# Another order at the last turns, in the first tail and before the first MLP group of a decoder block in Strassen-Winograd form

## The chip, the cores and the metric

The kernel runs on one core of a Trainium2 chip. The metric is the device time in microseconds, the median of several executions. The engines are TensorE (PE in the profile: matrix products and transposes), VectorE (DVE), ScalarE (ACT), GpSimd (POOL) and SyncE (SP). SP and POOL also issue the DMA transfers, each in a queue of its own that works in order.

## The reference

One layer (`DEPTH = 1`) on 512 tokens of width 2048, all float32. What matters, cut to its lines:

```python
h = rmsnorm(x, g_mix[l])
z = jnp.einsum('bsd,dc->bsc', h, w_in[l])
cb, cc, cv, q, k, v, f_logit, gate_c, gate_a = jnp.split(z, SPLIT_POINTS, axis=-1)
conv_y = cb * causal_dwconv(cc * cv, conv_w[l])
conv_branch = jnp.einsum('bsc,cd->bsd', conv_y, w_conv_out[l])
attn_branch = jnp.einsum('bsc,cd->bsd', forgetting_attention(q, k, v, log_f), w_attn_out[l])
merged = gc * conv_branch + ga * attn_branch
x = x + jnp.einsum('bsd,de->bse', merged, w_mix_out[l])
h = rmsnorm(x, g_mlp[l])
u = jnp.square(jax.nn.relu(jnp.einsum('bsd,df->bsf', h, w_ff1[l])))
x = x + jnp.einsum('bsf,fd->bsd', u, w_ff2[l])
return rmsnorm(x, g_final)
```

## The kernel before

**Products.** Every large product is done in 2 x 2 blocks with seven block products instead of eight, named A11, A12, S1, S2, S3, S4 and A22. Their operands are blocks or sums of blocks, of the activations (made once and kept as `ST`, `Q1`, `Q2` or `M`) and of the weights (made on VectorE for each group, lines L125 and L128). Each operand is split in a high part (a copy to a shorter format on ScalarE, `high_of`, L111, tiles `th`) and a low part (the rest, a subtraction on VectorE, `low_of`, L114, tiles `tl`). A block product is three rounds of matmuls: high by high, high by low, then low by high; so TensorE wants the high part of the weights at once and their low part after two thirds of the product (`mm_cols`) or of its first half (`mm_rows`).

**Groups.** A `Group` is one set of output columns. It loads four weight blocks X[i, j] of 1 MB each. `head` does A11 and A12, `tail`, `tail2` and `tail3` the other five in different orders. `run` splits an operand, queues its matmuls and then calls what is entered for that product in `after`. Four weight buffers x0 to x3 are passed on through the list `free`; two buffers each serve `th` and `tl`.

**Order.** The instructions are written in program order, and a planner then orders each engine's queue: of the instructions that are ready by its simulated times it takes the earliest in the program. `tied` (while `strict` is set) and `tc.keep_in_program_order` pin an instruction behind everything written before it on its engine; `tc.issue_after(i)` puts what follows behind `i` on i's engine, without waiting for its end. An engine executes its queue in the planner's order, whatever is ready on the chip.

**The three places.** (1) At the start, the rows of x come in four blocks `xin[0..3]`. Blocks 2 and 3 are scaled by their norm's factors r2 and r3 (made on GpSimd, L649; scaled at L731 and L732), turned by 32 transposes in eight steps of four (`turn_both`, L542, over the PSUM banks 6, 7, 2, 5), and copied out with the gain by `gained_both` (L550 on VectorE, L552 on ScalarE). Then the first key group's A11 begins. (2) The first group, `gV0`, has done A11 and A12 by then; its tail comes after the key groups' heads. Into it falls the split of the activations' S4 operand, `fourth`, entered behind S3. (3) The output projection's last group (g = 3, `tail3`) is followed by the first MLP group `g0`, whose weights come through GpSimd's queue (`g0.ahead`). Behind each product of the last group stand steps: `g0.ahead(i, j)` loads a block; `begin_part(n, k)` loads the first six eighths of an activation operand, which wait in memory; `split_part` splits A11's and A12's. `mix.first_of`, `mix.sums` and `mix.out` make the last two eighths of S1, S3, S2, S4 and A22 from the last group's own turned output. The lines that change there are these:

```python
g0.after = Steps(A11=[lambda: g0.ahead(1, 1), turn_waiting, begin_rest, lambda: first_sum_after(mix.added), mix.first_of],
                 A12=[lambda: mix.out("S1", mix.s1), mix.sums, lambda: factors(common, turned)])
```

Of the kernel before, what the change touches and what calls it, by code (L numbers as in the profile page):

```python
# [8 lines left out]
F32 = mybir.dt.float32  # L9
# [36 lines left out]
def tile_hybrid_block(ctx: ExitStack, tc, x, g_mix, w_in, b_f, b_gate, conv_w, w_conv_out,  # L46
# [69 lines left out]
    def split(src, hi, lo):  # L116
        return high_of(src, hi), low_of(src, hi, lo)

    def split_in_order(*how):

        for i in split(*how):
            tc.keep_in_program_order(i)

    def sub(out, a, b):
        return nc.vector.tensor_tensor(out=out, in0=a, in1=b, op=ALU.subtract)  # L125

    def add(out, a, b):
        nc.vector.tensor_tensor(out=out, in0=a, in1=b, op=ALU.add)  # L128

    def parts(shape, at=0):  # L130

# [72 lines left out]
    class Group:  # L204
# [3 lines left out]
        def __init__(self, view, c1, c2, w, ST, mm, banks, put, scale=1.0, extra={}, after=None, shift=SHIFT):  # L208
            self.extra, self.after, self.shift = extra, {} if after is None else after, shift
            self.view, self.cs, self.w, self.ST, self.mm, self.banks = view, (c1, c2), w, ST, mm, banks  # L210
            self.put, self.scale, self.at = put, scale, {}
            self.begun, self.queue, self.X = False, nc.sync, {}
            self.pinned, self.mid, self.apart, self.ready = False, {}, False, {}
            self.nq = view.shape[0] // (2 * P)

        def load(self, i, j):
# [12 lines left out]
            return [bank(i, which) for i in self.banks["abcd".index(which)]]  # L229

        def run(self, ps, n, src, first):
            if n in self.ready:
                hi, lo = self.ready.pop(n)
            else:
                hi, lo = self.places()
                split(src, hi, lo)
            if n in self.mid:
                self.mm(ps, self.ST(n), hi, lo, first, blocks=(0,))
                self.mid[n]()
                self.mm(ps, self.ST(n), hi, lo, first, blocks=(1,))  # L240
# [19 lines left out]
        def plus(self, s, ps, scale=1.0):  # L260

            if len(ps) == 1:
                pairs = [(s, ps[0][:, :2 * self.w].rearrange("p (b c) -> p b c", b=2))]
            else:
                pairs = [(s[:, b, :], ps[b][:, :self.w]) for b in range(2)]
            for o, p in pairs:
                if scale == 1.0:
                    add(o, p, o)
                else:
                    nc.vector.scalar_tensor_tensor(out=o, in0=p, scalar=scale, in1=o, op0=ALU.mult, op1=ALU.add)  # L270

        def done(self, *ij):
            free.append(self.at.pop(ij))
# [75 lines left out]
        def first_sum(self, pinned=True):  # L349
# [4 lines left out]
            if pinned:  # L354
                tc.keep_in_program_order(one)

        def tail2(self):

            X = self.quarters((0, 1), (0, 0), (1, 1), (1, 0))
            a = self.a  # L360
            if not self.pinned:
                sub(X[0, 0], X[0, 1], X[0, 0])
            c = self.acc("c")
            self.run(c, "S1", X[0, 0], True)
            third = sub(X[0, 1], X[1, 1], X[0, 1])
            if self.pinned:
# [4 lines left out]
            sub(X[two], X[1, 1], X[0, 0])  # L371
            self.done(*other)
            d1 = self.snap(d, self.scale, (1, 1))
            self.plus(d1, c, self.scale)
            while later:
                later.pop(0)()
            self.run(a, "S2", X[two], False)
            sub(X[1, 0], X[1, 0], X[two])
            self.done(*two)
            s2 = self.snap(a, ij=(1, 0))  # L380
            self.plus(d1, a, self.scale)
            self.put(1, 1, d1)
            self.run(c, "S4", X[1, 1], False)
            self.done(1, 1)
            s4 = self.snap(c, self.scale, (0, 1))
            self.plus(s4, a, self.scale)
            self.put(0, 1, s4)
            self.run(d, "A22", X[1, 0], False)
            self.done(1, 0)
            self.plus(s2, d)  # L390
            self.put(1, 0, s2)


        def tail3(self):

            X = self.quarters((0, 1), (0, 0), (1, 1), (1, 0))
            a = self.a
            sub(X[0, 0], X[0, 1], X[0, 0])
            c = self.acc("c")
            self.run(c, "S1", X[0, 0], True)  # L400
            sub(X[0, 0], X[1, 1], X[0, 0])
            d1 = self.snap(c)
            self.run(a, "S2", X[0, 0], False)
            sub(X[1, 0], X[1, 0], X[0, 0])
            self.done(0, 0)
            s2 = self.snap(a)
            self.plus(d1, a)
            self.run(c, "S4", X[1, 1], False)
            sub(X[0, 1], X[1, 1], X[0, 1])
            self.done(1, 1)  # L410
            s4 = self.snap(c)
            self.plus(s4, a)
            self.put(0, 1, s4)
            d = self.acc("d")
            self.run(d, "S3", X[0, 1], True)
            self.done(0, 1)
            self.plus(d1, d)
            self.put(1, 1, d1)
            self.plus(s2, d)
            self.run(a, "A22", X[1, 0], True)  # L420
            self.done(1, 0)
            self.plus(s2, a)
            self.put(1, 0, s2)

# [65 lines left out]
    class Quarters:  # L490
# [51 lines left out]
                    tied(nc.tensor.transpose(pt[:, k, e * P:(e + 1) * P], xin[t][:, c * P:(c + 1) * P], ident))  # L542
            return pt

        def gained_both(self, i, cs, pt):

            for k, c in enumerate(cs):
                o, g = self.H[i, k][:, c // 2, :], self.gT[:, c:c + 1]
                if c & 2:
                    tied(nc.vector.tensor_scalar(out=o, in0=pt[:, k, :], scalar1=g, scalar2=None, op0=ALU.mult))  # L550
                else:
                    tied(nc.scalar.activation(out=o, in_=pt[:, k, :], func=AF.Copy, scale=g))  # L552

        def sums(self):
            H = self.H
# [172 lines left out]
    high_of(*A12[:2])  # L728
    low_of(*A12)
    tied(nc.scalar.activation(out=cols[:, KT:], in_=pv[:, :NV - KT], func=AF.Copy))  # L730
    tied(nc.vector.tensor_scalar(out=xin[2], in0=xin[2], scalar1=r2, scalar2=None, op0=ALU.mult))  # L731
    tied(nc.scalar.activation(out=xin[3], in_=xin[3], func=AF.Copy, scale=r3))  # L732
# [7 lines left out]
    Q1.tiles("A22")  # L740
    for n in range(KT // 2):
        cs = (2 * n, 2 * n + 1)
        Q1.gained_both(1, cs, Q1.turn_both((2, 3), cs, (6, 7, 2, 5)[n % 4]))
    low_of(keys.X[0, 0], hi3, lo3)
    keys.ready["A12"] = hi4, lo4 = keys.places()
    high_of(keys.X[1, 0], hi4)
    low_of(keys.X[1, 0], hi4, lo4)
    strict[0] = False
    s1 = gV0.snap(gV0.a)
    gV0.plus(s1, b)  # L750
    gV0.done(0, 0)
    gV0.done(1, 0)
    gV0.put(0, 0, s1)
# [11 lines left out]
        Q1.last_sum("S4", (0, 1))  # L765
        strict[0] = False

    gV0.after["S3"] = fourth
    for g in heads:
        g.tail2()  # L770
        if g is gV0:
# [157 lines left out]
    n = 0  # L929
# [273 lines left out]

    def split_part(n):
        lo = Q2[n][:, 1, :KT // 2 - 2]
        split_in_order(lo.bitcast(F32), Q2[n][:, 0, :KT // 2 - 2], lo)

    class Mix:

# [58 lines left out]

        def first_of(self):
            self.s1 = pm.tile([P, 2, HS], F32, tag="s1", name="s1")  # L1270
            add(self.s1, self.F[1][:, 0], self.F[1][:, 1])

        def sums(self):
            (a11, a12), (a21, a22) = ([f[:, par] for par in range(2)] for f in self.F)
            s1 = self.s1
            sub(a21, a11, a21)
# [90 lines left out]
    for g in range(4):  # L1367
# [16 lines left out]
            after.add("S2", mix.fourth)  # L1384
        else:
            after.add("A12", lambda: begin_part("A11", 0))
            after.add("S4", lambda: g0.ahead(0, 0), lambda: begin_part("S1", 1))
            after.add("S4", lambda: split_part("A11"))
            after.add("S3", lambda: g0.ahead(1, 0), lambda: begin_part("S3", 3))
            after.add("A22", lambda: g0.ahead(0, 1))  # L1390
            after.add("A22", lambda: split_part("A12"))
        group = groups[g]
# [2 lines left out]
            after.add("A11", group.first_sum)  # L1395
        if g == 3:
            group.mid["A22"] = turn_first
        group.head(True, between=groups[1].first if g == 0 else lambda: None)
        (group.tail2 if g < 3 else group.tail3)()
        before = mix  # L1400

    def begin_rest():
        for n, k in (("S2", 5), ("S4", 6), ("A22", 2)):
            begin_part(n, k)

    def first_sum_after(ins):
        with tc.issue_after(ins.ins):
            g0.first_sum(pinned=False)

    def factors(common, r):  # L1410

# [267 lines left out]
```

## Time and profile before

| | us |
|---|---|
| runs (3), lowest, median, highest | 2431.68, 2435.55, 2437.17 |
| profiled execution, device time | 2433.25 |
| its span, first to last instruction | 2431.4 |
| TensorE busy | 2404.7 |
| VectorE busy | 2041.5 |
| ScalarE busy | 1201.7 |
| GpSimd busy | 299.4 |

A row of the order of time begins with the start and the length in us, then engine, line, operation, out<-in, shape and count; in brackets stands the idle time of the engine before it and what ended it. A row of the list of waits has the waiting instruction, what it waited for, the sum in us, how often, and the longest. A row of a table of stretches has the stretch, its length, each engine's busy time with its instructions in brackets (PE, weight loads, DVE, ACT, POOL), the granted TensorE clock as a share of full speed, the DMA engines' mean share and their GB/s. A row of the DMA issues ends with the KB of one and the us from issue to landing.

### The profile page before, as it was taken

How to read it: one execution, taken by the hardware profiler on the slowest of the kernel's cores; microseconds unless marked ns; L12 is line 12 of the kernel's file. 1: busy time of each engine (PE TensorE's matmuls, PEld its weight loads, DVE VectorE, ACT ScalarE, POOL GpSimd, SP SyncE). 2: the span in 40 equal slices, each digit the busy share in tenths (PEclk: the TensorE clock that was granted, in tenths of full speed). 3: DMA queues.
4: the chain of work that ended last, by engine and by line, in shares of the span. 5: the costliest groups of instructions: out<-in, count | busy, mean ns of one | idle time of the engine just before them, and what ended most of it. 6: DMA issues, size and time to landing. Idle time of an engine off the chain costs nothing.

```text
span 2431.4 us, 41446 instructions
## 1 busy us (share of the span) xinstructions
PE 2404.7 (99%) x17783; PEld 2262.7 (93%) x17783; DVE 2041.5 (84%) x1739; ACT 1201.7 (49%) x1230; POOL 299.4 (12%) x480
## 2 busy tenths in 40 slices
PE   9999999999999999999999999999999999999998
PEld 9999999999999999899899999999998888888886
DVE  7987777788887778888889889898887888889898
ACT  6444434445555534356566666666665333333334
POOL 1100111111111112023300000000011001100000
PEclk9999999999999999999999999999999999999999
DMA  8564554464656755657855565655678567655662
GB/s 265 181 201 147 151 160 139 139 193 150 203 186 199 241 176 191 208 177 236 306 200 188 203 231 190 230 180 210 220 291 290 169 225 243 224 202 184 237 228 101
DMA packets 279847, 491.98 MB, mean 202 GB/s; under 512 B 11820, under 2 KB 191112, under 8 KB 279280
## 3 DMA queue, kind: packets, MB, share of 16 engines
q1 hardware_dynamic: 226384, 272.71, 35.5%
q0 software_dynamic: 52672, 215.57, 24.2%
q8 instruction: 139, 2.28, 0.4%
q10 hardware_dynamic: 608, 1.06, 0.1%
q14 instruction: 44, 0.36, 0.0%
HBM read 379.70 MB, written 109.07 MB: 201 GB/s over the span
## 4 chain that ended last, share of the span: by engine, by line
PE 86%; DVE 5%; issue 3%; DMA 3%; ACT 1%; POOL 1%; SPq 0%; DVEq 0%; POOLq 0%; ACTq 0%
PE a L165 6%; PE a L169 6%; PE a L167 6%; PE a L188 5%; PE d L165 5%; PE a L186 5%; PE a L184 5%; PE d L167 5%; PE d L169 5%; PE c L165 4%; PE c L167 4%; PE c L169 4%; PE d L188 3%; PE d L186 3%; PE d L184 3%
## 5 line engine op out<-in xcount | busy, mean ns | idle before, releaser
L111 ACT ACTIVATE th<-x 128x2048 fp32r<-128x2048 f32 (+1 forms) x280 | 536.8, 1918 | 508.2 <-DVE x L125 160.4
L114 DVE TENSOR_TENSOR tl<-x,th 128x2048 fp32r<-128x2048 f32 (+2 forms) x282 | 639.0, 2271 | 165.4 <-ACT th L111 154.4
L125 DVE TENSOR_TENSOR x<-x,x 128x2048 f32<-128x2048 f32 (+1 forms) x160 | 365.6, 2285 | 26.4 <-DMA x<-in_w_in_dram 18.9
L111 ACT ACTIVATE th<-y 128x2048 fp32r<-128x2048 f32 (+1 forms) x109 | 185.4, 1702 | 274.1 <-PE a L186 138.8
L114 DVE TENSOR_TENSOR tl<-y,th 128x2048 fp32r<-128x2048 f32 (+1 forms) x109 | 218.8, 2012 | 30.0 <-ACT th L111 29.5
L184 PE MATMUL a<-th,us 128*128 128x512 f32 x512 | 199.3, 389 | 1.0 <-ACT th L111 1.0
L186 PE MATMUL a<-th,us 128*128 128x512 f32 x512 | 199.2, 389 | 0.0
L165 PE MATMUL c<-S,th 128*128 128x256 f32 x848 | 196.4, 277 | 0.6 <-ACT th L111 0.6
L167 PE MATMUL c<-S,th 128*128 128x256 f32 x848 | 196.5, 277 | 0.0
L165 PE MATMUL a<-S,th 128*128 128x256 f32 x784 | 181.3, 277 | 0.0
L167 PE MATMUL a<-S,th 128*128 128x256 f32 x784 | 180.8, 277 | 0.0
L165 PEld LDWEIGHTS c<-S,th 128*128 128x128 f32 x848 | 159.4, 188 | 0.7 <-ACT th L111 0.7
L167 PEld LDWEIGHTS c<-S,th 128*128 128x128 f32 x848 | 159.4, 188 | 0.2 <-issue 0.2
L167 PEld LDWEIGHTS a<-S,th 128*128 128x128 f32 x784 | 147.3, 188 | 0.0
L165 PEld LDWEIGHTS a<-S,th 128*128 128x128 f32 x784 | 147.2, 188 | 0.0
L188 PE MATMUL a<-tl,us 128*128 128x512 f32 x512 | 136.9, 389 | 0.6 <-DVE tl L114 0.6
L165 PE MATMUL d<-S,th 128*128 128x256 f32 x544 | 127.4, 279 | 0.0
L167 PE MATMUL b<-A,th 128*128 128x256 f32 x544 | 127.4, 279 | 0.0
L167 PE MATMUL d<-S,th 128*128 128x256 f32 x544 | 126.9, 278 | 0.0
L165 PE MATMUL a<-A,th 128*128 128x256 f32 x544 | 126.8, 278 | 0.0
L165 PE MATMUL b<-A,th 128*128 128x256 f32 x544 | 126.1, 277 | 0.0
L167 PE MATMUL a<-A,th 128*128 128x256 f32 x544 | 126.1, 277 | 0.0
(398 smaller groups left out, 6063.7 us busy)
## 6 DMA issues: line engine op xcount, KB each, us to landing
x<-in_w_in_dram SPq DMA_DIRECT2D x86, 1024.0 KB, 6.2
y<-in_w_ff_dram SPq DMA_DIRECT2D x64, 1024.0 KB, 7.7
x<-in_w_ff_dram SPq DMA_DIRECT2D x60, 1024.0 KB, 8.3
us<-s_d POOLq DMA_DIRECT2D x48, 1024.0 KB, 9.3
s_d<-rh POOLq DMA_DIRECT2D x32, 896.0 KB, 5.5
s_d<-r POOLq DMA_DIRECT2D x32, 896.0 KB, 6.1
x<-in_w_mix_out_dram SPq DMA_DIRECT2D x17, 1024.0 KB, 7.0
g_d<-o POOLq DMA_DIRECT2D x32, 256.0 KB, 2.7
```

What stands on the lines that cost most here:

```text
L111: return tied(nc.scalar.activation(out=hi, in_=src, func=AF.Copy))
L114: return tied(nc.vector.tensor_tensor(out=lo, in0=src, in1=hi.bitcast(F32), op=ALU.subtract))
L125: return nc.vector.tensor_tensor(out=out, in0=a, in1=b, op=ALU.subtract)
L165: nc.tensor.matmul(o, hi[:, q, js], Sh, start=first and q == 0 and j == 0, stop=False, skip_group_check=True)
L167: nc.tensor.matmul(o, hi[:, q, js], Sl, start=False, stop=False, skip_group_check=True)
L169: nc.tensor.matmul(o, lo[:, q, js], Sh, start=False, stop=q == nq - 1, skip_group_check=True)
L184: tied(nc.tensor.matmul(o, Sh, hi[:, q, :], start=begin and q == 0, stop=False, skip_group_check=True))
L186: tied(nc.tensor.matmul(o, Sl, hi[:, q, :], start=False, stop=False, skip_group_check=True))
L188: tied(nc.tensor.matmul(o, Sh, lo[:, q, :], start=False, stop=q == nq - 1, skip_group_check=True))
```

## The change

(1) Block 2 is scaled on ScalarE and block 3 on VectorE, the other way round than before. The steps 0, 1, 3 and 6 of the eight copies go to VectorE and the others to ScalarE (before: the odd ones to VectorE), and the sum `gV0.plus(s1, b)` is put behind step 3's copy. (2) `fourth` is entered behind S2 instead of S3, and what S4's run puts on VectorE (its low part) is put behind `half`, the sum of S3 and S1. (3) `tail3` splits S2's operand and makes S4's high part before S2's matmuls are written. In the last group's steps the loads of S1's and S3's parts leave their places: `g0.ahead(1, 1)` and S1's part now come right behind A22 (`freed`), S3's with the others in `begin_rest`. `early_sums`, entered behind A12 of `g0`, writes out VectorE's order for the three differences of weights (S1, S3, S2), the low parts of S1 and S3 and the two parts of the activations, the first behind the low part of A12's activations.

```diff
         def run(self, ps, n, src, first):
-            if n in self.ready:
+            if n in self.half:
+                hi, lo = self.half.pop(n)
+                low_of(src, hi, lo)
+            elif n in self.ready:
                 hi, lo = self.ready.pop(n)
...
+        def early_sums(self, before, between):
+
+            self.pinned = self.summed = True
+            X = self.quarters((0, 1), (1, 1))
+            with tc.issue_after(before.ins):
+                tied(sub(X[0, 0], X[0, 1], X[0, 0]))
+            between[0]()
+            self.ready["S1"] = hi, lo = self.places()
+            high_of(X[0, 0], hi)
+            tied(sub(X[0, 1], X[1, 1], X[0, 1]))
+            between[1]()
+            self.ready["S3"] = high, low = self.places()
+            high_of(X[0, 1], high)
+            low_of(X[0, 0], hi, lo)
+            tied(sub(X[0, 0], X[1, 1], X[0, 0]))
+            low_of(X[0, 1], high, low)
...
-            self.run(c, "S4", X[1, 1], False)
+            if self.paced:
+                with tc.issue_after(half.ins):
+                    self.run(c, "S4", X[1, 1], False)
+            else:
+                self.run(c, "S4", X[1, 1], False)
...
@@ tail3
             d1 = self.snap(c)
+            self.ready["S2"] = hi, lo = self.places()
+            split(X[0, 0], hi, lo)
+            self.half["S4"] = hi, lo = self.places()
+            high_of(X[1, 1], hi)
             self.run(a, "S2", X[0, 0], False)
...
             self.done(1, 0)
+            self.freed()
             self.plus(s2, a)
...
-    tied(nc.vector.tensor_scalar(out=xin[2], in0=xin[2], scalar1=r2, scalar2=None, op0=ALU.mult))
-    tied(nc.scalar.activation(out=xin[3], in_=xin[3], func=AF.Copy, scale=r3))
+    tied(nc.scalar.activation(out=xin[2], in_=xin[2], func=AF.Copy, scale=r2))
+    tied(nc.vector.tensor_scalar(out=xin[3], in0=xin[3], scalar1=r3, scalar2=None, op0=ALU.mult))
...
-        Q1.gained_both(1, cs, Q1.turn_both((2, 3), cs, (6, 7, 2, 5)[n % 4]))
+        last = Q1.gained_both(1, cs, Q1.turn_both((2, 3), cs, (6, 7, 2, 5)[n % 4]), n in (0, 1, 3, 6))
+        if n == 3:
+            third = last
...
-    gV0.plus(s1, b)
+    with tc.issue_after(third.ins):
+        gV0.plus(s1, b)
...
-    gV0.after["S3"] = fourth
+    gV0.after["S2"] = fourth
+    gV0.paced = True
...
-    g0.queue = nc.gpsimd
+    g0.queue, g0.apart = nc.gpsimd, True
...
-            after.add("S4", lambda: g0.ahead(0, 0), lambda: begin_part("S1", 1))
+            after.add("S4", lambda: g0.ahead(0, 0))
             after.add("S4", lambda: split_part("A11"))
-            after.add("S3", lambda: g0.ahead(1, 0), lambda: begin_part("S3", 3))
+            after.add("S3", lambda: g0.ahead(1, 0))
...
+            group.freed = lambda: (g0.ahead(1, 1), begin_part("S1", 1))
...
-        for n, k in (("S2", 5), ("S4", 6), ("A22", 2)):
+        for n, k in (("S3", 3), ("S2", 5), ("S4", 6), ("A22", 2)):
             begin_part(n, k)
-    def first_sum_after(ins):
-        with tc.issue_after(ins.ins):
-            g0.first_sum(pinned=False)
+    def first_parts():
+        mix.first_of()
+        mix.out("S1", mix.s1)
+        mix.second_of()
+
+    def in_order():
+        strict[0] = True
+        g0.early_sums(parted["A12"], (first_parts, lambda: mix.out("S3", mix.F[1][:, 0])))
+        strict[0] = False
...
-    g0.after = Steps(A11=[lambda: g0.ahead(1, 1), turn_waiting, begin_rest, lambda: first_sum_after(mix.added), mix.first_of],
-                     A12=[lambda: mix.out("S1", mix.s1), mix.sums, lambda: factors(common, turned)])
+    g0.after = Steps(A11=[turn_waiting, begin_rest],
+                     A12=[in_order, lambda: mix.sums(False), lambda: factors(common, turned)])
     g0.head(True)
-    for n in SPLIT[1:]:
+    for n in SPLIT[2:]:
         mix.out(n, mix.parts[n])
```

More of the change, by code (lines that the diff above doesn't have):

```diff
@@ L117, in split, with split_in_order @@
         return high_of(src, hi), low_of(src, hi, lo)
-    def split_in_order(*how):
+    parted = {}
+    def split_in_order(*how, kept=None):
         for i in split(*how):
             tc.keep_in_program_order(i)
+            parted[kept] = i
     def sub(out, a, b):
@@ L127, in add @@
     def add(out, a, b):
-        nc.vector.tensor_tensor(out=out, in0=a, in1=b, op=ALU.add)
+        return nc.vector.tensor_tensor(out=out, in0=a, in1=b, op=ALU.add)
     def parts(shape, at=0):
@@ L213, in __init__ @@
             self.pinned, self.mid, self.apart, self.ready = False, {}, False, {}
+            self.freed, self.summed, self.paced, self.half = lambda: None, False, False, {}
             self.nq = view.shape[0] // (2 * P)
@@ L267, in plus @@
                 if scale == 1.0:
-                    add(o, p, o)
+                    i = add(o, p, o)
                 else:
-                    nc.vector.scalar_tensor_tensor(out=o, in0=p, scalar=scale, in1=o, op0=ALU.mult, op1=ALU.add)
+                    i = nc.vector.scalar_tensor_tensor(out=o, in0=p, scalar=scale, in1=o, op0=ALU.mult, op1=ALU.add)
+            return i
         def done(self, *ij):
@@ L364, in tail2 @@
             self.run(c, "S1", X[0, 0], True)
-            third = sub(X[0, 1], X[1, 1], X[0, 1])
-            if self.pinned:
+            if not self.summed:
+                third = sub(X[0, 1], X[1, 1], X[0, 1])
+            if self.pinned and not self.summed:
                 tc.keep_in_program_order(third)
@@ L370, in tail2 @@
             two, other = ((0, 0), (0, 1)) if self.apart else ((0, 1), (0, 0))
-            sub(X[two], X[1, 1], X[0, 0])
+            if not self.summed:
+                sub(X[two], X[1, 1], X[0, 0])
             self.done(*other)
             d1 = self.snap(d, self.scale, (1, 1))
-            self.plus(d1, c, self.scale)
+            half = self.plus(d1, c, self.scale)
             while later:
@@ L543, in turn_both, with gained_both @@
             return pt
-        def gained_both(self, i, cs, pt):
+        def gained_both(self, i, cs, pt, vector):
             for k, c in enumerate(cs):
                 o, g = self.H[i, k][:, c // 2, :], self.gT[:, c:c + 1]
-                if c & 2:
-                    tied(nc.vector.tensor_scalar(out=o, in0=pt[:, k, :], scalar1=g, scalar2=None, op0=ALU.mult))
-                else:
-                    tied(nc.scalar.activation(out=o, in_=pt[:, k, :], func=AF.Copy, scale=g))
+                if vector:
+                    last = tied(nc.vector.tensor_scalar(out=o, in0=pt[:, k, :], scalar1=g, scalar2=None, op0=ALU.mult))
+                else:
+                    last = tied(nc.scalar.activation(out=o, in_=pt[:, k, :], func=AF.Copy, scale=g))
+            return last
         def sums(self):
@@ L1205, in split_part @@
         lo = Q2[n][:, 1, :KT // 2 - 2]
-        split_in_order(lo.bitcast(F32), Q2[n][:, 0, :KT // 2 - 2], lo)
+        split_in_order(lo.bitcast(F32), Q2[n][:, 0, :KT // 2 - 2], lo, kept=n)
     class Mix:
@@ L1270, in first_of, with second_of, sums @@
             self.s1 = pm.tile([P, 2, HS], F32, tag="s1", name="s1")
-            add(self.s1, self.F[1][:, 0], self.F[1][:, 1])
-        def sums(self):
+            tied(add(self.s1, self.F[1][:, 0], self.F[1][:, 1]))
+        def second_of(self):
+            tied(sub(self.F[1][:, 0], self.F[0][:, 0], self.F[1][:, 0]))
+        def sums(self, second=True):
             (a11, a12), (a21, a22) = ([f[:, par] for par in range(2)] for f in self.F)
             s1 = self.s1
-            sub(a21, a11, a21)
+            if second:
+                self.second_of()
             sub(a11, s1, a11)
```

## The prediction

> **What bounds the kernel now.** I read the page first, then TensorE's own list of waits, then the order of time on each engine around the places that the change touches.
>
> ```profile
> PE 2404.7 (99%) x17783; PEld 2262.7 (93%) x17783; DVE 2041.5 (84%) x1739; ACT 1201.7 (49%) x1230; POOL 299.4 (12%) x480
> ...
> PE d L158 <- ACT th L111: 2.3, 2, 2.1
> PE c L169 <- DVE tl L114: 1.4, 1, 1.4
> PE ptr L542 <- ACT h L552: 1.2, 1, 1.2
> ```
>
> TensorE (PE) is busy for 99% of the span, so nothing but its holes can be won: 2431.4 less 2404.7 is 26.7 us, start and end included. The list of its waits (what waits, for whom, us in total, times, longest) has the places of this change near its top: the turns (ptr L542) and the first MLP group (d L158, c L169). Matmuls queue behind each other, so a hole that goes shortens the run by its length, unless the next input is late too. A change of 0.2%, 4.9 us, is about what a measurement of this kernel can tell from none: the three runs themselves spread from 2431.68 to 2437.17.
>
> **Part 1, the turns of row blocks 2 and 3.** PE's rows, then the other engines':
>
> ```profile
> 29.00 0.27 PE L542 MATMUL ptr<-ident,xn 128*128 128x128 f32 x1
> 29.90 1.86 PE L542 MATMUL ptr<-ident,xn 128*128 128x128 f32 x15 [0.63 <-ACT xn L732]
> 32.91 0.66 PE L542 MATMUL ptr<-ident,xn 128*128 128x128 f32 x4 [1.16 <-ACT h L552]
> 33.78 1.50 PE L542 MATMUL ptr<-ident,xn 128*128 128x128 f32 x12 [0.21 <-DVE h L550]
> 35.03 0.37 PE L165 MATMUL a<-A,th 128*128 128x256 f32 x1
> ```
> ```profile
> 25.36 2.45 POOL L649 TENSOR_TENSOR r<-v,mhalf 128x1 f32<-128x1 f32 x1 [0.87 <-DVE v L643]
> ...
> 26.48 1.28 DVE L731 TENSOR_SCALAR xn<-xn,r 128x2048 f32<-128x2048 f32 x1
> ...
> 25.21 0.21 ACT L730 ACTIVATE cols<-pv 128x72 f32<-128x72 f32 x1
> 27.84 2.01 ACT L732 ACTIVATE xn<-xn,r 128x2048 f32<-128x2048 f32 x1 [2.41 <-POOL r L649]
> 29.75 1.90 ACT L111 ACTIVATE th<-x 128x2048 fp32r<-128x2048 f32 x1
> 31.55 0.57 ACT L253 ACTIVATE o<-a 128x512 f32<-128x512 f32 x1
> 32.03 2.41 ACT L552 ACTIVATE h<-ptr,cols 128x256 f32<-128x256 f32 x6
> ...
> 32.76 3.43 DVE L550 TENSOR_SCALAR h<-ptr,cols 128x256 f32<-128x256 f32 x8
> ```
>
> From the first transpose to the first matmul of the next group are 6.03 us. Fifteen transposes take 1.86, the last 0.27 of it, so one follows the other each 0.11, and 32 need 3.5: 2.5 us are lost. ScalarE (ACT) is the cause: it waits 2.41 for the second factor r, scales block 3 until 29.85, then makes the high part th until 31.65, and only then empties the first bank of transposes.
>
> With the two scalings exchanged, ACT begins block 2 at 25.4 (at the latest 26.5, when DVE has that factor here) and ends at 27.4; th is done at 29.3. VectorE (DVE) gets block 3: factor at 27.8 at the latest, plus 1.28, is 29.1, which is when its first transpose is due (29.00 + 0.11). The POOL row covers DVE's work from 26.48, so the factor may come sooner; then there is slack. The first two banks now go to DVE, idle then: a copy each 0.41 (3.43 by 8), so bank 0 is free at 29.6 + 0.9 = 30.5 against PE's need at 29.0 + 16 x 0.11 = 30.8, and the second at 31.3 against 31.2. ACT takes the third from 30.5. I leave 0.2 for such waits: gain **2.3** (2.5 if none is left; 1.3 if ACT's o<-a, 0.57, and the sum that follows it fall between the copies twice). DVE and ACT have the same number of copies as before and end them some 2 us sooner, so the work behind them moves along. The weights' loads behind it start when DVE has read a buffer, hence move with it.
>
> **Part 2, the first tail.**
>
> ```profile
> 84.22 2.29 DVE L114 TENSOR_TENSOR S<-h,S 128x2048 fp32r<-128x2048 f32 x1
> 86.42 4.61 DVE L125 TENSOR_TENSOR x<-x,x 128x2048 f32<-128x2048 f32 x2
> 90.95 4.48 DVE L114 TENSOR_TENSOR tl<-x,th 128x2048 fp32r<-128x2048 f32 x2
> ...
> 90.79 0.38 PE L184 MATMUL a<-th,S 128*128 128x256 f32 x1 [0.66 <-ACT th L111]
> ...
> 93.28 0.38 PE L188 MATMUL a<-tl,S 128*128 128x256 f32 x1 [0.40 <-DVE tl L114]
> ```
>
> The split of S4's moving operand (S<-h, 2.2 to the next start) stands on DVE ahead of S2's difference. Moved behind S2, it lets the difference end at 86.5 and its high part at 88.5; the next difference fills DVE until 88.7, the low part ends at 90.9. PE wants them at 90.0 and 91.8, so both waits go: 0.66 + 0.40, and 0.17 more for each, since a matmul is drawn 0.28 long and the next may start after 0.11: **1.4**. Next late would be S4: PE wants its operand at 90.0 + 5.4 = 95.4. DVE: its low part 91 to 93.1, the sum `half` 0.7, then the paced low part of the weights 2.3, ending at 96.1 where PE wants it 1.8 after 95.4. What waits behind the paced instruction on DVE is the next group's difference only. One more 2.2 us operation in between would cost 1; hence 0.4 to 1.4 here.
>
> **Part 3, the first MLP group.**
>
> ```profile
> 1200.38 0.28 PE L1418 MATMUL mean<-ms,ones 128*128 128x4 f32 x2
> 1201.30 0.39 PE L165 MATMUL c<-S,th 128*128 128x256 f32 x1 [0.64 <-ACT th L111]
> 1206.62 2.10 PE L169 MATMUL c<-S,tl 128*128 128x256 f32 x16 [1.40 <-DVE tl L114]
> 1210.82 0.35 PE L158 MATMUL d<-S,th 128*128 128x192 f32 x1 [2.11 <-ACT th L111]
> ...
> 1211.00:1215.00 4.00, 4.00 (x22) 4.00 (x23) 4.00 (x3) 1.01 (x2) 0.00 (x0) 0.57 0.00 0
> ```
> ```profile
> 1193.12 1.76 DVE L114 TENSOR_TENSOR A<-A 128x1536 fp32r<-128x1536 f32 x1 [1.01 <-ACT A L111]
> ...
> 1197.02 2.28 DVE L125 TENSOR_TENSOR x<-x,x 128x2048 f32<-128x2048 f32 x1
> ...
> 1202.47 1.89 DVE L114 TENSOR_TENSOR S<-f,S 128x512 fp32r<-128x512 f32 x3
> 1204.28 2.29 DVE L114 TENSOR_TENSOR tl<-x,th 128x2048 fp32r<-128x2048 f32 x1
> 1206.48 2.29 DVE L125 TENSOR_TENSOR x<-x,x 128x2048 f32<-128x2048 f32 x1
> ...
> 1194.87 0.83 ACT L1251 ACTIVATE f<-ptr,cols 128x256 f32<-128x256 f32 x2
> ...
> 1185.41 0.92 POOL L222 DMA_DIRECT2D x<-in_w_ff_dram  x1
> 1190.20 0.71 POOL L1226 DMA_DIRECT2D x_d<-o  x1 [3.88 <-DVE o L1225]
> 1190.91 0.90 POOL L222 DMA_DIRECT2D x<-in_w_ff_dram  x1
> ...
> x<-in_w_ff_dram POOLq DMA_DIRECT2D x1, 1024.0 KB, 11.3
> ```
>
> The idle is 0.64 + 1.40 + 2.11 = 4.15, with 3 x 0.17 at the edges. After the last hole the granted clock is 0.57 over 4 us (column PEclk): 4 x 0.43 = 1.7 us more. Together 6.4.
>
> All three waits are DVE's order: the first difference starts at 1197.02 behind smaller work (its weights land at 1185.41 + 11.3 = 1196.7), the low part at 1204.28 behind eight small operations, S3's difference at 1206.48.
>
> The fixed order, with 2.2 for a large operation and 0.6 for a small one (three in 1.89) between starts: first difference 1194.8 (behind A12's low part); s1 at 1197.0 (its inputs are there at 1195.7); ACT splits s1 until 1198.4, then th until 1200.2, where PE wants it at 1200.5: that wait goes, with 0.3 to spare. DVE: s1's low part 1198.4, F's difference 1199.0, S3's difference 1199.6 to 1201.9, F's low part 1201.8, S1's low part 1202.4 to 1204.7. PE wants that at 1200.5 + 32 x 0.115 = 1204.2, so 0.5 + 0.2 = **0.7 stays**. S3's high part is done at 1203.8 (wanted 1206.7), S2's difference 1206.9, S3's low part 1209.1 (wanted 1210.4). Then the sum of b, two sums and three splits wait on DVE, some 4 us, and S2's own low part ends near 1215.4, wanted 1216.0. No idle of 2 us is left, so the clock should stay up. Gain 6.4 - 0.7 = **5.7**; between 3.3 (one more large operation ahead of S1's low part) and 6.4.
>
> This needs the weights sooner. The two 1.5 MB parts that go on POOL's queue ahead of them now come behind; at the rate of the row below they are 8 us of queue:
>
> ```profile
> 1179.00:1187.00 8.00, 8.00 (x73) 8.00 (x72) 7.24 (x7) 4.01 (x7) 3.79 (x5) 1.00 1.03 393
> ```
>
> So the first lands near 1189, against 1194.8. The second was issued at 1190.91, behind a store that waits for a sum; ahead of that store it lands by 1192, behind it near 1197, against 1199.6. The parts, 4 us each, then land from 1195 (at worst 1201) on: S1 wanted at 1200.5, S3 at 1206.7, the rest later. Worst 0.5 us. In the last Mix group the earlier split of S2 and S4's earlier high part change no wait that I can find; the 1.15 us hole there may go or double: nothing counted.
>
> Sum: 2.3 + 1.4 + 5.7 = **9.4**. The profiled execution took 2433.25 (span 2431.4) and would come to 2423.9; the median of the runs, 2.3 above it, to **2426.2**.
>
> [...] In this trace the clock halved behind a hole of 2.11 us. [...]
>
> **The rivals.** [...] (b) The fixed order only moves the waits: two large operations ahead of S1's low part, or its high part late by as much, take back 4.4 and with the clock's 1.7 leave about 3.3: 2432.3, no change that can be told. For it: DVE has no idle time from 1193 to 1209 in my order; against: each step was counted from rows. (c) Slower: the instructions' order is planned by simulated times, so the attention stage behind part 1 may be interleaved anew. Its place is the 32 softmax blocks on PE:
>
> ```profile
> PE sc L828 <- DVE m L832: 0.8, 3, 0.3
> ```
>
> Only 3 of 32 wait there for a maximum, 0.3 at the longest. If each waited 0.3, that is 9.6 and the gain is gone; from 0.45 each (14.4 less 9.4) the run is slower by over 0.2%, 2440.6. Against it: all engines reach that stage some 3 us sooner together, and no line of it is touched. (d) The loads keep their places on POOL's queue: first difference at 1196.7, all of part 3 later by 1.9, saving 7.5 and 2428.1.
>
> **How the numbers follow.** Forecast 0.50; (a) 0.18; (d) 0.11; (b) 0.13; (c) 0.08. The first three are faster by over 0.2%: 0.79. Same is (b) 0.13, slower (c) 0.08. The range leaves out (c) and half of (b)'s tail: below, 9.4 + 0.7 + 1.15 and some 3 us of the runs' spread give 2421.5; above, (b) gives 2432.5.
>
> **What would show it.** Right: ptr L542 without waits over 0.3 and L165 near 32.7; no wait of a L184 and L188 in the first tail; c L165 with no wait, c L169 with about 0.5, d L158 with none and PEclk 1.00 there; the x loads landing before 1195. Wrong: a new wait of PE over 1 us in these stages, or longer waits of sc L828.

## The result, and the profile after

The changed kernel took 2424.83 us (median of 6 runs, 2424.09 to 2428.01) against 2435.32 (6 runs, 2430.68 to 2437.17), which is 10.5 us less between the medians. The ratio of the runs is 0.9963, interval 0.9950 to 0.9976, so the saving is some 0.4%, 5.8 to 12.2 us. Two later series gave 2423.46 against 2433.84 (ratio 0.9960, 0.9948 to 0.9973) and 2425.14 against 2433.57 (0.9961, 0.9948 to 0.9973). The forecast was 2426.2. The profiled executions took 2425.45, 2423.24 and 2425.14; there the forecast was 2423.9.

The page and TensorE's list of waits after the change:

```profile
PE 2401.9 (99%) x17783; PEld 2260.7 (93%) x17783; DVE 2041.3 (84%) x1739; ACT 1202.6 (50%) x1230; POOL 299.9 (12%) x480
...
PE d L187 <- ACT th L111: 2.5, 1, 2.5
...
PE c L187 <- ACT o L260: 1.2, 1, 1.2
PE sc L869 <- DVE m L873: 1.0, 3, 0.6
```

The waits of the turns and of the first MLP group are gone. What leads the list now lies elsewhere: A22 of an output projection group near 1098 us (2.5, before 1.75), and the hole near 1166 that stood before too (1.2, before 1.15). The attention's three waits for a maximum stay.

The turns, in the order of time on PE, POOL, DVE and ACT:

```profile
28.86 2.35 PE L578 MATMUL ptr<-ident,xn 128*128 128x128 f32 x20
30.96 0.36 PE L168 MATMUL a<-A,th 128*128 128x256 f32 x1
31.31 1.50 PE L578 MATMUL ptr<-ident,xn 128*128 128x128 f32 x12
32.56 0.37 PE L170 MATMUL a<-A,th 128*128 128x256 f32 x1
```
```profile
25.22 1.62 POOL L686 TENSOR_TENSOR r<-v,mhalf 128x1 f32<-128x1 f32 x1 [0.88 <-DVE v L680]
...
26.87 1.29 DVE L769 TENSOR_SCALAR xn<-xn,r 128x2048 f32<-128x2048 f32 x1 [0.44 <-POOL r L686]
...
25.18 2.00 ACT L768 ACTIVATE xn<-xn,r 128x2048 f32<-128x2048 f32 x1
```

The 32 transposes run without a wait; one matmul of the next group was drawn between them, and that group goes on at 32.56. The second factor took 1.62 us here against 2.45 before.

The first tail, PE and DVE:

```profile
87.37 0.28 PE L187 MATMUL a<-th,S 128*128 128x256 f32 x1
...
89.26 1.11 PE L191 MATMUL a<-tl,S 128*128 128x256 f32 x8
...
81.56 4.62 DVE L128 TENSOR_TENSOR x<-x,x 128x2048 f32<-128x2048 f32 x2
86.09 2.28 DVE L114 TENSOR_TENSOR tl<-x,th 128x2048 fp32r<-128x2048 f32 x1
88.30 2.28 DVE L114 TENSOR_TENSOR S<-h,S 128x2048 fp32r<-128x2048 f32 x1
```

Neither S2 nor its low part waits any more, and S4's split stands behind S2's.

The first MLP group, PE, DVE, the two late weight loads and S1's part on POOL's queue, and the table of stretches:

```profile
1200.24 0.28 PE L1470 MATMUL mean<-ms,ones 128*128 128x4 f32 x2
1200.38 0.36 PE L168 MATMUL c<-S,th 128*128 128x256 f32 x1
...
1204.41 2.15 PE L172 MATMUL c<-S,tl 128*128 128x256 f32 x16
1206.40 0.25 PE L161 MATMUL d<-S,th 128*128 128x192 f32 x1
```
```profile
1194.46 2.28 DVE L128 TENSOR_TENSOR x<-x,x 128x2048 f32<-128x2048 f32 x1
...
1202.07 2.29 DVE L114 TENSOR_TENSOR tl<-x,th 128x2048 fp32r<-128x2048 f32 x1
...
1180.53 0.92 POOL L226 DMA_DIRECT2D x<-in_w_ff_dram  x1
...
1185.06 0.90 POOL L226 DMA_DIRECT2D x<-in_w_ff_dram  x1
1185.95 0.71 POOL L1241 DMA_DIRECT2D S<-h_d  x1
...
S<-h_d POOLq DMA_DIRECT2D x1, 1536.0 KB, 13.9
...
1211.00:1215.00 4.00, 4.00 (x38) 4.00 (x37) 4.00 (x7) 3.17 (x4) 0.00 (x0) 1.00 0.89 285
```

S1's high part is in time and S3's too; only the low part is missed, by 0.15 us. The clock stays at 1.00. S2 of this group begins at 1211.98 instead of 1218.23. One cover is thin: S1's part, issued at 1185.95, lands 13.9 us later at 1199.8, and its first use is at 1200.38. In the second series' profiled execution it came too late, and PE waited 0.37 us for it.

### The profile page after: what moved, and what is told of

Same layout as the page of the kernel before. It is cut to its first block, busy times and chain, and to the rows that moved or that the text cites. A ratio compares the mean times of both kernels' runs of the same rounds, so it can differ in the third digit from the quotient of the medians.

```text
span 2423.6 us, 41438 instructions
## 1 busy us (share of the span) xinstructions
PE 2401.9 (99%) x17783; PEld 2260.7 (93%) x17783; DVE 2041.3 (84%) x1739; ACT 1202.6 (50%) x1230; POOL 299.9 (12%) x480
## 4 chain that ended last, share of the span: by engine, by line
PE 86%; DVE 4%; issue 4%; DMA 3%; ACT 1%; POOL 1%; SPq 0%; DVEq 0%; POOLq 0%; ACTq 0%
PE a L168 6%; PE a L172 6%; PE a L170 6%; PE a L189 5%; PE a L187 5%; PE a L191 5%; PE d L168 5%; PE d L170 5%; PE d L172 5%; PE c L168 4%; PE c L170 4%; PE c L172 4%; PE d L191 3%; PE d L189 3%; PE d L187 3%
```

## The experiments

**Each part alone.** Part 1 on the kernel before:

```diff
-    tied(nc.vector.tensor_scalar(out=xin[2], in0=xin[2], scalar1=r2, scalar2=None, op0=ALU.mult))
-    tied(nc.scalar.activation(out=xin[3], in_=xin[3], func=AF.Copy, scale=r3))
+    tied(nc.scalar.activation(out=xin[2], in_=xin[2], func=AF.Copy, scale=r2))
+    tied(nc.vector.tensor_scalar(out=xin[3], in0=xin[3], scalar1=r3, scalar2=None, op0=ALU.mult))
...
```

> Only part 1 of the change (the two scalings exchanged, the copies' new shares, the sum of b behind the third), on the kernel before. The prediction has 2.3 us for it: about 2433.0 against 2435.3, L578's transposes in one piece and the next group's first matmul near 32.8 us. Rival: the waits come back later in the same stage (the sum of b or the first tail), then within 0.5 us of before. [...]

Measured: 2432.03 against 2433.93, ratio 0.9991 (0.9982 to 1.0001): as forecast, though the runs alone don't tell it from nothing. Part 2 alone:

```diff
-    gV0.after["S3"] = fourth
+    gV0.after["S2"] = fourth
+    gV0.paced = True
```

> Only part 2 (the split of S4's moving operand behind S2, S4's low part behind the half sum). The prediction has 1.4 us for it: 2433.9, with no wait at the S2 product of the first tail. Rival, from the trace after: matmuls there follow each other every 118 ns instead of 113 until about 139 us where the stall is gone (529 of them, against 145 before), so 384 x 4.7 ns = 1.8 us come back and the run is within 0.5 us of before. [...]

Measured: 2434.28 against 2433.93, ratio 1.0004 (0.9995 to 1.0013): nothing won, as the rival has it, which was written from the trace after. Two instructions serve as marks: the 192-column matmul ahead of S3 in the first two key groups. Their rows (first and last start at the end of the counts) of before, part 1 alone, part 2 alone and the changed kernel:

```profile
L158 PE MATMUL d<-S,th x2: 248/250/252, 113.6 to 140.9; 128*128 128x192 f32 x2
```
```profile
L161 PE MATMUL d<-S,th x2: 249/251/253, 110.8 to 138.1; 128*128 128x192 f32 x2
```
```profile
L161 PE MATMUL d<-S,th x2: 252/252/252, 112.3 to 140.7; 128*128 128x192 f32 x2
```
```profile
L161 PE MATMUL d<-S,th x2: 252/252/253, 110.0 to 138.4; 128*128 128x192 f32 x2
```

Part 1 is 2.8 us ahead at both marks. Of this, 0.16 stood there before the first transpose (28.84 against 29.00), and 0.18 came in the tail, where its stall ahead of S2 is 0.48 and not 0.66; so the turns won 2.45. Part 2 is 1.2 ahead at the first mark and 0.2 at the second, and 0.24 of that stood there before the tail, whose first matmul starts at 78.42 against 78.66. It reaches S4 at 95.38 against 97.02: by then the tail has won 1.4, and by the second mark all of it is given back. The whole change shows the same, 3.6 and then 2.5. From mark to mark are 27.3 us in the three traces without part 2 (before, part 1, part 3) and 28.4 in all eight that have it and no added matmul. Where it goes is seen in the mean duration of PE's groups (the number behind the busy time, ns), from 94 to 107 us, of before and of part 2 alone:

```profile
L184 PE MATMUL c<-th,S 128*128 128x256 f32 x16 | 3.7, 276 | 0.0
```
```profile
L187 PE MATMUL c<-th,S 128*128 128x256 f32 x16 | 3.9, 281 | 0.0
```

Matmuls drawn with 276 ns start 113 ns apart, those with 281 start 118 apart. In the kernel before, the 118 pace began with this tail at 78.7 and ended at 91.0, behind the stall of 0.66 us that part 2 removes; another 50 matmuls had it later, 145 in all. Without the stall it runs on to the second mark: 529 matmuls. 384 more by 4.7 ns are 1.8 us. This is no chance of one execution: all eight traces with part 2 have some 530 slow matmuls there, and the three without it, with stalls of 0.48 to 0.68 us ahead of S2, have some 145. The test for it puts one 192-column matmul ahead of S3 in this tail, on part 2 alone:

```diff
-    gV0 = Group(..., store_v(0, VW), shift=3 * SHIFT)
+    gV0 = Group(..., store_v(0, VW), shift=3 * SHIFT, extra={"S3": "first"})
```

> Part 2 alone, with one matmul of 192 columns ahead of the S3 product of the first tail. If part 2 by itself won nothing because the 118 ns pace then ran on to 139 us, the slow matmuls in that stage fall from 529 to some 50 and part 2 gains its 1.4 us and some 0.4 more: 2432.1 against 2433.9, and the trace has about 1.0 us of excess from 50 to 150 us instead of 2.7. If part 2's gain was lost elsewhere, 2434 as without the short matmul.

Measured: 2432.37 against 2433.57, ratio 0.9997 (0.9989 to 1.0006). The counts of PE's matmuls in two stretches, of before, part 2, and part 2 with the short matmul:

```profile
88.00:100.00 12.00, 10.94 (x94) 10.54 (x93) 9.22 (x6) 6.60 (x5) 0.85 (x1) 1.00 0.79 233
100.00:150.00 50.00, 50.00 (x442) 50.00 (x441) 44.00 (x26) 19.71 (x14) 6.23 (x9) 1.00 0.64 196
```
```profile
88.00:100.00 12.00, 12.00 (x105) 12.00 (x104) 11.48 (x7) 6.92 (x6) 2.82 (x2) 1.00 0.81 240
100.00:150.00 50.00, 50.00 (x430) 50.00 (x429) 41.97 (x25) 19.83 (x14) 6.22 (x9) 1.00 0.64 198
```
```profile
88.00:100.00 12.00, 12.00 (x105) 12.00 (x104) 11.49 (x7) 7.29 (x6) 2.82 (x2) 1.00 0.79 231
100.00:150.00 50.00, 50.00 (x439) 50.00 (x438) 42.27 (x25) 20.15 (x15) 6.22 (x9) 1.00 0.65 202
```

Part 2 wins 11 matmuls in the first stretch and loses 12 in the second. The short matmul ahead of S3 did not end the slow pace at once, but it ended at 113.4, with the first mark, instead of 141.3 with the second, after 288 matmuls instead of 529, and 9 of the 12 came back, 1.0 us. From mark to mark it takes 27.3 us again. In the traces the loss is thus shown to be the pace. The runs point the same way, with overlapping intervals.

On the changed kernel, with the short matmul ahead of S1 and of S3 there:

> The changed kernel with one more matmul of 192 columns at the head of the S1 and of the S3 product of the first tail (it writes what the next matmul overwrites; 0.09 us each). If the 118 ns from matmul to matmul are a state that the stall ended before and that a short matmul can end too, the 529 slow matmuls from 76 to 139 us shrink to some 50, which is 479 x 4.7 ns = 2.2 us less 0.2: 2422.8. Rival: the pace hangs on the operands' places in that stage; it stays at 118 and the run is 0.2 us longer, 2425.0.

Measured: 2422.84, ratio to before 0.9955 (0.9942 to 0.9967), beside the changed kernel's 0.9960 in the same series: no difference that these runs can tell. That the median is the expected one is luck, since what was expected did not happen: the slow pace did not stop after some 50 matmuls. The first of the two did not end it and the second did, at 84.7; but this execution had been in it since 33.3. Up to 78 us the order on PE, DVE, ACT and POOL is that of the changed kernel, so no difference of order explains this early start. With seven such matmuls, six of them in the output projection:

> The changed kernel with a matmul of 192 columns ahead of S3 in the first tail and ahead of A11 and S3 in output projection groups 1 to 3, seven in all (0.09 us each). In the changed kernel's second profile 529 matmuls from 76 to 139 us and some 480 from 1071 to 1187 us had the pace of 118 ns. If six in ten of these go back to 113: 600 x 4.7 ns = 2.8 less 0.6, so 2421.5. If the state comes back at once, 2424.2.

Measured: 2425.36 against 2425.14 for the changed kernel: missed. The slow pace stood from 33.0 to 78.4, before the first of the seven, and came several times in the output projection.

**Part 3 and what in it counts.** Part 3 alone:

> Only part 3 (the weights' loads sooner, the fixed order of VectorE, the last group's splits). The prediction has 5.7 us for it: 2429.6, no wait over 0.3 us from 1200 to 1216 us and PEclk 1.00 there. If the fixed order gains nothing by itself and the rest of the saving is interplay of the parts, under 3 us. If the halved clock comes from another hole's length as in the profile after (2.5 us near 1098 us), that hole decides whether an execution has 0.998 or 0.999.

Measured: 2427.14 against 2433.93, ratio 0.9975 (0.9967 to 0.9984): 6.8 us between the medians, 3.9 to 8.0 by the interval. It is most of the change. From 1200 to 1216 us PE is idle for 0.15 and the clock is 1.00. Then the changed kernel with the loads back in their places:

```diff
-            after.add("S4", lambda: g0.ahead(0, 0))
+            after.add("S4", lambda: g0.ahead(0, 0), lambda: begin_part("S1", 1))
...
-            after.add("S3", lambda: g0.ahead(1, 0))
+            after.add("S3", lambda: g0.ahead(1, 0), lambda: begin_part("S3", 3))
...
-            group.freed = lambda: (g0.ahead(1, 1), begin_part("S1", 1))
...
```

> The changed kernel with the loads of the first MLP group's weights and of S1's and S3's parts back in the places of before; the fixed order stays. The prediction's case (d): the first difference at 1196.7 minus the 2.3 us that part 1 wins instead of 1194.5, all of it later by 1.9 us, so 2426.7 against 2424.8. Rival: VectorE stands still behind the fixed first difference, and the small operations behind it (s1, the split of its low part) are late too, and the second load lands only after a store that waits: then the waits of 4.1 us and the halved clock of 1.7 come back, 2430 or more. Third: the loads didn't matter, since the planner's order alone made the difference late before: 2424.8.

Measured: 2427.23, ratio to before 0.9973 (0.9961 to 0.9984). The weights' load on POOL, DVE's first difference and PE's S1:

```profile
1183.68 0.92 POOL L226 DMA_DIRECT2D x<-in_w_ff_dram  x1
...
1194.79 0.69 DVE L114 TENSOR_TENSOR A<-f,A 128x512 fp32r<-128x512 f32 x1 [1.44 <-ACT A L111]
1195.40 2.28 DVE L128 TENSOR_TENSOR x<-x,x 128x2048 f32<-128x2048 f32 x1
...
1200.80 0.39 PE L168 MATMUL c<-S,th 128*128 128x256 f32 x1 [1.77 <-ACT th L111]
```

The mean's matmul stands at 1198.75 here, 1.5 us earlier than in the changed kernel's profile, so by that measure the difference is 2.4 us later, and PE waits 1.77 for it. In size that is case (d) of the prediction, 1.9 there. But the transfer itself is less than half of it. It takes 10.4 us and lands at 1194.1, which by the same measure is 1.1 us later than the changed kernel's start of the difference. The rest is order: here a small low part of the activations (A<-f) stands ahead of the difference on DVE and waits 1.44 for ACT; in the changed kernel it stands behind. That the planner turned the two round because of the later load is likely, but not shown. The runs agree with it (2.4 more than 2424.83, though of another series) but don't settle it alone.

Now the early loads without the fixed order:

```diff
-        g0.early_sums(parted["A12"], (first_parts, lambda: mix.out("S3", mix.F[1][:, 0])))
+        with tc.issue_after(ins.ins):
+            g0.first_sum(pinned=False)
...
```

> The changed kernel without the fixed order of VectorE before the first MLP group; the weights still come early and the last group keeps its splits. Parts 1 and 2 stay. The prediction has the waits as VectorE's order: then most of 1.4 and 2.1 us comes back, and with the halved clock, where a hole of 2 us falls into one window, some 5 us: 2430. Rival, that the loads were late and set the order: the three waits stay away and the run is within 1 us of the changed kernel.

Measured: 2432.01 against 2433.84, ratio 0.9992 (0.9983 to 1.0001): nearly all is lost.

```profile
1197.13 0.55 PE L168 MATMUL c<-S,th 128*128 128x256 f32 x1 [4.25 <-DMA S<-h_d]
...
1196.00:1203.00 7.00, 5.87 (x28) 5.91 (x29) 4.35 (x8) 2.52 (x4) 1.05 (x1) 0.51 1.02 424
```

But not in the way that either theory said. The planner made the first difference at 1187.68, and then drew five of S1's matmuls ahead of A12's on PE. They wait 4.25 us for S1's part, which now comes behind the weights and lands at 1197.0, and behind that the granted clock is halved for some 6.8 us (0.51 over the 7 us from 1196). The low part's wait of 1.4 is gone, S3's is 1.3. So early loads alone turn DVE's wait into one for a DMA; it takes the written order to use them. This run says nothing about the order with S1's part in time, since PE's order changed with DVE's.

The earlier splits in the last output projection group, taken out:

```diff
-            self.ready["S2"] = hi, lo = self.places()
-            split(X[0, 0], hi, lo)
-            self.half["S4"] = hi, lo = self.places()
-            high_of(X[1, 1], hi)
             self.run(a, "S2", X[0, 0], False)
```

> The changed kernel without the earlier split of S2's operand and without the earlier high part of S4's in the last output projection group. The prediction counted nothing for these: 2424 as the changed kernel, with the hole near 1166 us (0.75 to 1.2 us in the changed kernel) still there. Rival: they cost or save that hole, 1 us either way.

Measured: 2424.55, ratio to before 0.9961 (0.9948 to 0.9975), beside 0.9961 for the changed kernel in that series: nothing. The hole near 1166 has 2.0 us in this execution, and 0.75, 1.19 and 1.20 in the three of the changed kernel; but part 3 alone and the kernel with seven short matmuls have the splits and 2.2 us there, so the traces don't put it down to the splits.

**The hole near 1098.** In it PE waits for A22's high part, which stands on ACT behind a copy whose buffer is still being stored (in the changed kernel's first profile the copy starts at 1094.90, after 7.71 us of waiting for that store). Handing out two stores later:

```diff
+        if late:
+            after.add("A22", lambda: mixes[0].give("S3"), lambda: mixes[0].give("A22"))
         after.add("A22", turn_first)
...
-            for n, part in (("A12", "S1"), ("S1", "S3"), ("S2", "A22")):
+            for n, part in (("A12", "S1"),) if late else (("A12", "S1"), ("S1", "S3"), ("S2", "A22")):
```

> The changed kernel with two stores of the second output projection group's predecessor (its S3 and A22 parts) handed out behind A22 instead of behind S1 and S2, so that ScalarE makes A22's high part near 1092 us and doesn't stand behind a copy that waits for its buffer's last store. The hole of 1.65 to 2.6 us near 1098 goes, and with it any halved clock there (1.7 us in about two executions of three of those with 2.5): 2422.0. Rival: the stores pile up behind and the next group waits for them instead: 2424.8.

Measured: 2425.54, ratio 0.9965 (0.9952 to 0.9977): nothing gained, as the rival has it. The hole near 1098 is gone, but the wait only moved to the next turns:

```profile
PE ptr L1283 <- DVE o L1266: 2.2, 1, 2.2
```

**The changed kernel, twice more.**

> The changed kernel once more, as the measure for the three runs beside it: 2424.8. If one execution in several has a halved clock where a hole of 2.5 us near 1098 us falls whole into one 3.41 us window, the runs split into 2424 and 2426 or more.

> The changed kernel, as the measure for the three beside it: 2423.5 to 2424.8.

Measured: 2423.46 and 2425.14. The ten executions lie between 2421.29 and 2426.84, without the two groups expected. Their profiled executions took 2423.24 and 2425.14, the first one 2425.45. The two slower ones have the clock halved behind the hole near 1098, the quicker one has not.

**The clock, from all fourteen traces.** The mean clock of an execution, given to three digits, does not tell what I had expected of it: it was 0.998 in two executions whose traces have no halved stretch inside. The traces do tell. Wherever the clock changes in a trace, the times lie whole multiples of 3.413 us apart: in that of before they are 1211.04, 1214.46 and 2426.19 us, with 1 and 355 such steps between them, in the first of the changed kernel 1098.24, 1101.65 and 2419.20, with 1 and 386. So the whole trace can be cut into windows of that length. The stretches of before (a halving), of the changed kernel (a halving), of part 1 (none, at two holes), and of part 3 (none, then a halving), cut at those windows:

```profile
1207.63:1211.04 3.41, 1.30 (x12) 1.11 (x11) 1.38 (x2) 2.18 (x2) 0.00 (x0) 1.00 0.67 276
1211.04:1214.45 3.41, 3.41 (x18) 3.41 (x18) 3.41 (x3) 0.97 (x2) 0.00 (x0) 0.50 0.00 0
```
```profile
1094.83:1098.24 3.41, 0.88 (x9) 0.68 (x7) 1.42 (x3) 3.13 (x4) 2.14 (x4) 1.00 0.92 341
1098.24:1101.65 3.41, 3.41 (x16) 3.41 (x17) 3.38 (x3) 3.41 (x5) 0.00 (x0) 0.50 0.59 224
```
```profile
1091.47:1094.88 3.41, 1.72 (x16) 1.51 (x14) 1.39 (x2) 2.18 (x3) 1.27 (x3) 1.00 0.97 364
1094.88:1098.29 3.41, 2.25 (x17) 2.05 (x18) 2.50 (x2) 3.41 (x5) 0.88 (x2) 1.00 0.76 282
...
1207.52:1210.93 3.41, 2.09 (x17) 2.09 (x18) 2.11 (x1) 2.52 (x3) 0.00 (x0) 1.00 0.06 25
1210.93:1214.34 3.41, 3.41 (x31) 3.41 (x30) 3.41 (x5) 0.80 (x1) 0.00 (x0) 1.00 0.00 0
```
```profile
1101.44:1104.85 3.41, 1.65 (x14) 1.65 (x15) 2.30 (x2) 3.41 (x5) 1.60 (x3) 1.00 0.85 317
1104.85:1108.26 3.41, 3.24 (x28) 3.03 (x27) 3.38 (x4) 2.83 (x6) 0.72 (x1) 1.00 0.44 120
...
1169.71:1173.12 3.41, 1.24 (x10) 1.05 (x10) 3.41 (x5) 3.24 (x7) 3.11 (x6) 1.00 0.77 276
1173.12:1176.53 3.41, 3.41 (x18) 3.41 (x17) 2.84 (x3) 0.72 (x2) 2.11 (x5) 0.50 0.88 248
```

PE's busy time is the first number after the length, PEclk the third from the end. Behind windows with 0.88, 1.24 and 1.30 us of work (2.53, 2.17 and 2.11 without matmuls) the clock is 0.50, behind those with 1.65 and 1.72 (1.76 and 1.69 without) it is 1.00. Part 1's hole near 1095 is longer (2.63 us) than before's at 1210 (2.11), but it lies across a border, 1.69 and 0.94. Its hole ahead of the first MLP group's S3 is 2.10 like before's, lies across a border too, 0.77 and 1.33, and no halving follows. Over the fourteen traces ten holes have 1.96 us or more inside one window, and each was followed by the halved clock. Ten others of 1.97 to 2.80 us are cut by a border into pieces of at most 1.77, and none was. One window more was halved in the kernel without the fixed order: it followed a window that was itself at half clock and had only some 1.0 us without matmuls. So these counts are of windows at full clock.

## Why the prediction was right, point by point

**Part 1** (2.3): 2.45 us in the trace, 1.9 in the runs (4.4 to -0.2 by the interval). The mechanism is as worked out, ACT's early th and DVE's first copies included. The term was a little small: the transposes ran without the 0.2 that I had left for waits.

**Part 2** (1.4): this step failed. Both waits went, S4 was in time, the order of DVE came out as written, and at S4's start the 1.4 were there; but the sum took the pace between matmuls as given. It had read 0.113 and 0.118 as one number ("0.11"), and so missed that a slower pace had ended behind the stall (at 91.0 us), which now runs on to 139 us. What the term brought by 141 us is nothing (0.2 at the mark less the 0.24 that stood there before), not 1.4.

**Part 3** (5.7): 6.8 us in the runs of part 3 alone. In the first profiles, before and after, the way from the mean's matmul (1200.38, 1200.24) to S2 (1218.23, 1211.98) got 6.1 us shorter, the halved clock's 1.7 included. The idle went as worked out: S1's high part in time, S3's in time, loads at 1189.4 (forecast near 1189) and 1196.1 (1192 or 1197). The second missed the sign given for being right, a landing before 1195, which did no harm, as its difference starts only at 1199.26. Two sizes were off. The low part ended at 1204.4 and not 1204.7, so PE idled 0.15 there, not 0.5. And the 1.7 for the halved clock is not a constant of the kernel before. From the counts above I estimate how often it comes: a hole of 2.1 us leaves 1.96 or 1.77 in one window when no border cuts off more than 0.14 or 0.33 of it, and if the borders are equally likely to lie anywhere, that is (3.41 - 2.10 + 0.28 to 0.66) / 3.41, about half of all executions. Of the four traces without part 3, three have the halving and part 1's has not. So by this estimate the term is worth some 0.9 on the mean, and in two of its three profiles the changed kernel lost 1.7 to the clock near 1098, where its hole was 2.5 to 3.0 us in all three and before's was 1.75.

**The sum** (9.4, forecast 2426.2) held: between the medians of the three series are 10.5, 10.4 and 8.4 us, by their ratios 9.0, 9.7 and 9.5. That it came so near is in part luck, since the errors are of both signs: part 2 gave 1.4 less, the clock some 0.8 less, part 1 some 0.2 more and the low part's wait 0.4 more. That makes 7.8; what the series have beyond it, some 1 to 3 us, I cannot assign. The parts alone add up to 8.3 (1.9 - 0.4 + 6.8), each with an interval of some 2 us either way, so there need be little left to explain. Matmuls at the slow pace outside the first tail differ between traces by more than that: some 1730 in the one trace of before, 850 to 1110 in the three of the changed kernel, at 4.7 ns each. The median forecast also rests on a median of before that stood 2.3 us above its profiled execution; later series have before at 2433.57 to 2433.93, and from there 9.4 less is 2424.2 to 2424.5.

**The rivals.** The halved clock's 1.7 us are weighed under part 3. (b), the waits only move: no, one of 0.15 us is left. (c), the attention stage planned anew: no; the planner's order there is the same in both kernels on every engine, and in the first profiles its waits for a maximum were three in each, 0.8 and 1.0 us in all. (d), the loads' places: the loads did leave them, and with them back a wait of 1.77 is there where 1.9 was forecast, though late landing is only a part of its cause.

## What to carry to other kernels

A hole's price is its length only if nothing else hangs on it: here a stall of 0.66 us stood at the end of a slower pace (118 ns against 113), and without it the 1.2 us that part 2 was ahead at 112 us were 0.2 at 141. What a hole near two microseconds costs in clock differed here with where a window's border fell (ten with 1.96 us or more inside one window were followed by the halved clock, 1.7 us, ten cut into pieces of at most 1.77 were not), so take it as a chance and not as a sum. And transfers issued earlier are worth what the written order makes of them: here the loads without it turned a wait of 1.40 us for VectorE into one of 4.25 for a DMA.

## What the runs showed of the hardware

- In these traces TensorE's matmuls of 256 columns follow each other at two paces, 113 ns from start to start where they are drawn with 276, and 118 where they are drawn with 281. In the first tail some 95 in a row had the slower one before (78.7 to 91.0 us), and some 530 in the eight traces with part 2 and no added matmul, over changes of operand and group. It was over behind the stalls of 0.48 to 0.68 us ahead of S2 (before, part 1, part 3), and behind some 192-column matmuls, while it stood on behind others (in the changed kernel's first profile it stood on behind the mark at 110.0 us and was over behind the one at 138.4). What starts and what ends it is not shown.
- Every change of the granted clock lies a whole multiple of 3.413 us from the others of its trace. Over the fourteen traces ten windows of that length, at clock 1.00 and with 1.96 us or more without matmuls, were each followed by one at 0.50 (3.41 x 0.50 = 1.7 us lost), among them before's with 2.11, part 3's with 2.17 and the changed kernel's with 2.53. Behind those with 1.77 or less none was halved between the start and the last matmuls, as behind part 3's with 1.76 and part 1's with 1.69. One window at 0.50 with some 1.0 us without matmuls was followed by another at 0.50. What happens between 1.77 and 1.96 is not shown.
